# Tiles of the weight ring at 4224 instead of 4096 bytes, and two constants given up, in a decoder-block kernel

## The chip, the cores and the metric

The kernel runs on one core of one Trainium2 chip. The metric is the device time of one execution in microseconds (us), as the median over several executions. TensorE (PE) multiplies matrices, VectorE (DVE) and ScalarE (ACT) do elementwise work, GpSimd (POOL) a little of it, and SyncE (SP) issues every transfer (DMA) of this kernel. SBUF is the memory on the core, 128 partitions wide; an address below is a byte offset inside a partition, the same in all of them.

## The reference

One decoder block on x of 1024 tokens by 1024 channels, in float32. Two token mixers run side by side on the same normalised, modulated h: a chunked state-space mixer (SSD) and differential attention; two sigmoid gates merge them. A gated convolutional feed-forward part with 2816 hidden channels follows.

```python
h = rms_norm(x, pre_norm1_w) * (1.0 + sc1) + sh1
z, xbc, dt_raw, q, k, v, gates = jnp.split(h @ w_in, IN_SPLITS, axis=-1)
y_ssd = ssd_branch(z, xbc, dt_raw, ...)
y_att = diff_attention_branch(q, k, v, ...)          # softmax under a causal mask, blocks of 128 queries
gate_ssd, gate_att = jnp.split(sigmoid(gates), 2, axis=-1)
merged = gate_ssd * (y_ssd @ w_ssd_o) + gate_att * (y_att @ w_attn_o)
x = x + g1 * rms_norm(merged @ w_out, post_norm1_w)
h2 = rms_norm(x, pre_norm2_w) * (1.0 + sc2) + sh2
u_gate, u_val = jnp.split(causal_dwconv(h2 @ w_up, ...), 2, axis=-1)
x = x + g2 * rms_norm((gelu(u_gate) * u_val) @ w_down, post_norm2_w)
```

sh1, sc1, g1, sh2, sc2 and g2 are the six parts of silu(c) @ w_ada + b_ada.

## The kernel before

Every large product is made of three matmuls in the fp32r format: each operand is split into a high and a low part, and high times high, high times low and low times high are added up in PSUM. The big projections are arranged as block products with seven instead of eight multiplications (lists `order` and `downs`), so the same work is done with sums of blocks. One matmul has 128 rows by 128 columns of weights (the stationary operand, brought in by a weight load of its own) and streams 512 columns of the moving operand past them. In the z part (`mm3` at L954, printed on L118 to L120) it streams 346 or 348 columns.

**Memory.** Four pools share a partition, in this order. `cq` holds small constants. `wp` is the weight ring: a tag `wraw` with 3 buffers for weights as they are loaded, `whi` and `wlo` with 4 each for their split halves, 11 tiles of 4096 bytes. `sp` holds 43 slots of 4096 bytes, given out by the class `Slots` for activations, operands and scratch. `cp` holds the remaining constants. In the built program the ring's tiles start at 2048 + 4096 i and the slots at 47104 + 4096 k, so all of them start at multiples of 2048, and the 128-column pieces within them at multiples of 512. The exceptions are the z weights: a ring tile for them holds two rows of 346 (or 348) floats, one behind the other, so that the second starts 1384 (or 1392) bytes into the tile. For a part of them a tile `zown` of two slots stands in, where the second row starts 2048 bytes in.

**Order of the work.** PE, DVE, ACT and, until attention begins, SP have their order written out by hand in Python (`tc.manual_schedule`). In the part with attention (from L1674) SP is not in that list, and a scheduler sets the order of its transfers. PE's streams of matmuls are interleaved with attention by `fill(n)`, which emits n groups of three matmuls of a dense product.

**The mask.** `masked_min` (L1457) adds the causal mask to a tile of scores and takes the row minimum in one DVE instruction. Its mask `mw` is a slot with 896 zeros followed by a 128x128 block, 0 where a key may be seen and 1e30 elsewhere. That block is loaded early into a constant `maskbig` (L688) and copied into `mw` by DVE (L1681), just ahead of the first scores; the zeros are a memset (L1680).

**The gate rows.** `ada_turn` (L935) transposes two rows of gate factors on PE, copies them from PSUM into a constant `growt` of 16 partitions by 128 floats (L938) and writes them to DRAM as `rowd` (L940), from where they are later read broadcast over all partitions.

Of the kernel before, what the change touches and what calls it, by code (L numbers as in the profile page):

```python
# [17 lines left out]
P = 128  # L18
D = 1024
S = 1024  # L20
HALF = 512
KD = D // P
# [11 lines left out]
NROW = 48 + 256  # L34


class Slots:
    def __init__(self, pool, n):
        self.pool = pool
        self.free_list = list(range(n))  # L40
        self.of = {}
# [22 lines left out]
def kernel(ctx: ExitStack, tc: tile.TileContext, a: dict, out: bass.AP, dbg=None):  # L64
    nc = tc.nc
    V, A, G, T, SP = nc.vector, nc.scalar, nc.gpsimd, nc.tensor, nc.sync

    cq = ctx.enter_context(tc.tile_pool(name="cq", bufs=1))
    wp = ctx.enter_context(tc.tile_pool(name="wp", bufs=1))
    sp = ctx.enter_context(tc.tile_pool(name="sp", bufs=1))  # L70
    cp = ctx.enter_context(tc.tile_pool(name="cp", bufs=1))
    pp = ctx.enter_context(tc.tile_pool(name="pp", bufs=1, space=bass.MemoryType.PSUM))
# [1 line left out]
    SL = Slots(sp, NSLOT)  # L74

    def const(name, shape, dtype=F32):
        pool = cq if name in ("cT", "nhalf", "growt", "adac", "gcol", "aexp", "ssy") else cp
        return pool.tile(shape, dtype, tag=name, name=name)

    pairs_of_banks = ExitStack()  # L80
# [53 lines left out]
    def load_x(i):  # L134
        SP.dma_start(xts[i], a["x"][i * P : (i + 1) * P, :])

    cT = const("cT", [P, KD])
    nhalf = const("nhalf", [P, 8])
    ident = const("ident", [P, P])
    ones = const("ones", [P, P])  # L140
    tri = const("tri", [P, P])
    maskbig = const("maskbig", [P, P])
    SP.dma_start(cT, a["cT"])
    load_x(0)
    SP.dma_start(ident, a["ident"])
# [231 lines left out]
    def x_load():  # L377
        if not x_loads:
            return
        n, m = x_loads.pop(0)  # L380
        kind, i, j = pairs[m]
        src = {"gs": ("w_gate", "w_gate"), "xbc": ("w_xbc", "w_xbc"), "qk": ("w_q", "w_k"), "rope": ("w_q", "w_k")}[kind]["fv".index(n)]
        t = xw[n, m] = wp.tile([P, 2, KH, P], F32, tag="wraw", name=f"xw{n}{m}", bufs=3)
        SP.dma_start(t.rearrange("p h k c -> p (h k c)"), a[src][(i, j)["fv".index(n)]])
# [43 lines left out]
    n_ada, n_ald = 0, 0  # L428
    adac = const("adac", [P, 4 * KD])
    gcol = const("gcol", [P, 2 * KD])  # L430
    growt = const("growt", [2 * KD, P])
    sh2c, a2c = adac[:, KD : 2 * KD], adac[:, 2 * KD : 3 * KD]
    ada_of = {}

# [121 lines left out]
    with tc.manual_schedule(engines={EN.PE, EN.DVE, EN.Activation, EN.SP}):  # L556
# [128 lines left out]
                x_load()  # L685
        SP.dma_start(rows, a["rows"].broadcast_to([P, NROW]))
        SP.dma_start(tri, a["tri"])
        SP.dma_start(maskbig, a["maskbig"])  # L688
        x_load()
        SL.put(diag, *[t for p_ in adat for t in p_], rrow, raw3, *xT.values())  # L690
        vev1 = SL.get("vev1", F32, (P, 2, HALF))
# [148 lines left out]
    sm2 = SL.get("sm2", F32, (P, 1024))  # L840
    dtr, dt, la, acum, ea, cd, dte, sp0_ = (sm1[:, n] for n in range(8))
    sp1_ = sm2[:, 256:384]
    cbm = sm2[:, 384:640].rearrange("p (g l) -> p g l", g=2)
    btok = sm2[:, 640:896].rearrange("p (g l) -> p g l", g=2)
    ev = [SL.get(f"ev{i}", F32, (P, 2, HALF)) for i in range(3)]
# [2 lines left out]
    aexp = const("aexp", [P, NH])  # L848
# [94 lines left out]
    with tc.manual_schedule(engines={EN.PE, EN.DVE, EN.Activation, EN.SP}):  # L943
        for t_, (c0, wdt) in enumerate(thirds):
# [4 lines left out]
            for i in range(8):  # L949
# [20 lines left out]
                n = wdt - lo  # L970
# [52 lines left out]
    ssy = const("ssy", [P, 8, 2])  # L1023
# [9 lines left out]
    def run_bg(n):  # L1033
        for _ in range(min(n, len(bg))):
            tag, f_ = bg.popleft()
            f_()
            finished.add(tag)
# [67 lines left out]
    def fill(n):  # L1105
        for _ in range(n):
            next(stream, None)
# [110 lines left out]
    def turn_y(c, g, bank=ps_wb):  # L1218
        ps = bank(f"ytr{c}_{g}")
        for q in range(4):  # L1220
            T.transpose(ps[:, q * P : (q + 1) * P], yt[c % 3][:, (4 * g + q) * P : (4 * g + q + 1) * P], ident)
        st = yst[2 * (c == 7) + g]
        p4 = ps.rearrange("p (k t) -> p k t", t=P)
        s4 = st.rearrange("p (k n) t -> p k n t", n=2)
        A.activation(s4[:, :, 0, :], p4, AF.Copy)
        V.tensor_tensor(s4[:, :, 1, :], p4, s4[:, :, 0, :].bitcast(F32), op=ALU.subtract)
        SP.dma_start(ytd[:, 8 * g : 8 * g + 8, c * P : (c + 1) * P], st.bitcast(F32))
# [119 lines left out]
    mw = SL.get("mw")  # L1347
# [86 lines left out]
    def load_heads(j):  # L1434
        b = j % 2
        last = 2 + ((j + 1) * 96 - 1) // P
        if last > 3 and ("low", "w_k", last, 1) not in finished:
            run_lows()
            assert ("low", "w_k", last, 1) in finished
        assert emitted["scores"] >= 8 * (j - 1) and emitted["values"] >= 8 * (j - 1)  # L1440
        if j > 0:
            for s in range(2):
                load_highs(2 * j + s, qst[b][s], kst[b][s])
                load_lows(2 * j + s, klo[b][s])
        for kt in range(8):
            SP.dma_start(vt[b][:, kt, :], vd[kt][:, j * P : (j + 1) * P])
# [227 lines left out]
    with tc.manual_schedule(engines={EN.PE, EN.DVE, EN.Activation, EN.Pool}):  # L1674
        for n in range(NFIRST - 6):
            fill(1)
            if n == 1:
                turn_y(6, 1, ps_wc)
                load_heads(0)
                V.memset(mw[:, : S - P], 0.0)  # L1680
                V.tensor_copy(mw[:, S - P :], maskbig)  # L1681
            elif n == 8:
                turn_y(7, 0)
            elif n == 9:
                turn_y(7, 1, ps_wc)
            run_bg(1 if n < 8 else 2)
# [951 lines left out]
```

## Time and profile before

| | |
|---|---|
| median of 3 runs | 1803.32 us (1803.09 to 1804.15) |
| profiled execution | 1805.74 us, of which 1803.9 us are the span from first to last instruction |
| granted TensorE clock in it | 0.998 |
| DVE, ACT, POOL busy | 76%, 51%, 6% of the span |
| transfers | 356.18 MB, 59.7% of what 16 DMA engines could be busy |

The page gives busy time per engine, a chain of work that ended last, and groups of equal instructions with their mean length and the idle time ahead of them. PE's matmuls overlap each other in the records: a matmul of 512 columns is listed with 389 ns while the next one starts earlier, so the pace is read from start to start in the timeline, not from the mean length. The timeline has the time of start in us, the length in us, the engine, the line, the operation with output and inputs, its shape, and the idle time before it with what ended it.

### The profile page before, as it was taken

The page shows a single profiled execution, that of the slowest core. Times are in us where ns is not written, and L with a number is a line of the kernel's source. Part 1 is how long each engine was busy: PE and PEld are TensorE (multiplying, and loading weights), DVE is VectorE, ACT ScalarE, POOL GpSimd, SP SyncE. Part 2 cuts the span into 40 slices and gives each one's busy share as a digit, 9 for nine tenths or more (in the row PEclk, how much of TensorE's full clock was granted, in tenths as well). Part 3 has the DMA queues.
Part 4 walks back from the last instruction along what each step waited for, and adds up shares of the span by engine and source line. Part 5 has one row for each costly group of instructions (what it writes and reads, how often), then busy time and mean ns, then how long its engine had stood idle before and what let it go on. Part 6 is the DMA issues. An engine that isn't in the chain of part 4 may idle for free.

```text
span 1803.9 us, 24533 instructions
## 1 busy us (share of the span) xinstructions
PE 1780.5 (99%) x8749; PEld 1493.3 (83%) x8749; DVE 1363.7 (76%) x2245; ACT 919.6 (51%) x1794; POOL 111.7 (6%) x110
## 2 busy tenths in 40 slices
PE   8999999999999999999999999999999999999998
PEld 6788888899877888888888888888888888888887
DVE  7896888976489777666667876679898888876545
ACT  4454444443457556665555443665554554564532
POOL 0000000000155400000000000100000000000001
PEclk9999999999999999999999999999999999999999
DMA  9565687678877886679842576413232223378754
GB/s 368 180 221 164 244 273 258 188 240 279 267 257 245 256 246 175 174 208 272 262 147 100 181 252 254 154 53 117 99 125 103 100 100 111 122 240 305 232 161 165
DMA packets 165322, 356.18 MB, mean 197 GB/s; under 512 B 16064, under 2 KB 64976, under 8 KB 165200
## 3 DMA queue, kind: packets, MB, share of 16 engines
q1 hardware_dynamic: 165200, 354.62, 59.7%
q8 instruction: 69, 1.13, 0.3%
q14 instruction: 53, 0.43, 0.1%
HBM read 248.83 MB, written 103.62 MB: 195 GB/s over the span
## 4 chain that ended last, share of the span: by engine, by line
PE 62%; DVE 4%; ACT 3%; DMA 2%; issue 1%; SPq 0%; POOL 0%; DVEq 0%; POOLq 0%; ACTq 0%
PE upx L2026 4%; PE upx L2025 4%; PE upx L2027 4%; PE o L1532 2%; PE dx L2418 2%; PE dx L2416 2%; PE dx L2417 2%; PE upy L2025 2%; PE upy L2026 2%; PE upy L2027 2%; PE dy L2418 2%; PE dy L2416 2%; PE dy L2417 2%; PE at L1519 2%; PE mix L2088 1%; PE mix L2087 1%
## 5 line engine op out<-in xcount | busy, mean ns | idle before, releaser
L2025 PE MATMUL upx<-t,wu_t 128*128 128x512 f32 x264 | 103.1, 391 | 0.5 <-DVE cv L2481 0.4
L2026 PE MATMUL upx<-t,wu_t 128*128 128x512 f32 x264 | 102.8, 390 | 0.2 <-DVE t L2143 0.2
L2027 PE MATMUL upx<-t,wu_t 128*128 128x512 f32 x264 | 102.7, 389 | 0.0
L1457 DVE CUSTOM_DVE_ANT_0 sc<-sc,mw 128x256 f32<-128x256 f32 (+7 forms) x128 | 96.1, 771 | 8.5 <-PE sc L1470 7.3
L1999 ACT ACTIVATE wu_t<-sab 128x512 fp32r<-128x512 f32 x57 | 34.1, 627 | 127.5 <-DVE sab L2016 127.5
L1520 ACT COPY aT<-at 128x512 f32<-128x512 f32 (+2 forms) x96 | 45.9, 478 | 95.3 <-PE at L1519 95.0
L97 DVE TENSOR_TENSOR g_lo<-gst,g_hi 128x1024 fp32r<-128x1024 f32 (+1 forms) x42 | 47.4, 1134 | 49.0 <-ACT g_hi L96 49.0
L1532 PEld LDWEIGHTS o<-vt,aT 128*128 128x128 f32 x576 | 76.0, 191 | 7.2 <-ACT aT L1520 1.8
L1532 PE MATMUL o<-vt,aT 128*128 128x128 f32 x576 | 79.9, 275 | 1.3 <-ACT aT L1520 1.3
L96 ACT ACTIVATE g_hi<-gst 128x1024 fp32r<-128x1024 f32 (+1 forms) x42 | 41.3, 989 | 65.1 <-DMA gst<-gld_s 37.4
L398 ACT ACTIVATE xw_t<-xsab 128x512 fp32r<-128x512 f32 x45 | 27.3, 627 | 92.5 <-DVE xsab L407 92.5
L423 PE MATMUL xx<-xt,xw_t 128*128 128x512 f32 x180 | 70.2, 390 | 0.0
L424 PE MATMUL xx<-xt,xw_t 128*128 128x512 f32 x180 | 70.0, 389 | 0.0
L425 PE MATMUL xx<-xt,xw_t 128*128 128x512 f32 x180 | 70.0, 389 | 0.0
L1469 PE MATMUL sc<-kst,qst 128*128 128x512 f32 (+2 forms) x192 | 66.0, 352 | 0.0
L1507 DVE RECIPROCAL rsm<-ssum 128x2 f32<-128x2 f32 x64 | 10.6, 166 | 72.6 <-ACT p L1498 39.7
L1470 PE MATMUL sc<-klo,qst 128*128 128x512 f32 (+2 forms) x192 | 63.2, 346 | 0.0
L2043 DVE SCALAR_TENSOR_TENSOR ug<-cg,vec,ug 128x1023 f32<-128x1023 f32 (+1 forms) x44 | 56.3, 1279 | 6.1 <-ACT ug L2042 5.3
L2003 DVE TENSOR_TENSOR wu_t<-sab,wu_t 128x512 fp32r<-128x512 f32 x57 | 39.3, 689 | 26.5 <-ACT wu_t L1999 26.5
L2025 PEld LDWEIGHTS upx<-t,wu_t 128*128 128x128 f32 x264 | 49.6, 188 | 11.7 <-DVE cv L2481 1.4
L2026 PEld LDWEIGHTS upx<-t,wu_t 128*128 128x128 f32 x264 | 49.6, 188 | 10.6 <-DVE t L2143 0.5
L1511 DVE SCALAR_TENSOR_TENSOR p<-p,coef,p 128x512 f32<-128x512 f32 (+2 forms) x96 | 56.5, 616 | 2.2
(580 smaller groups left out, 5797.2 us busy)
## 6 DMA issues: line engine op xcount, KB each, us to landing
adas<-in_w_ada SPq DMA_DIRECT2D x32, 512.0 KB, 5.8
wdr<-in_w_down SPq DMA_DIRECT2D x22, 512.0 KB, 4.9
wtd<-wdr SPq DMA_DIRECT2D x22, 512.0 KB, 3.3
wuf<-in_w_up SPq DMA_DIRECT2D x22, 512.0 KB, 3.4
gld_s<-gsum SPq DMA_DIRECT2D x22, 512.0 KB, 2.8
gst<-gld_s SPq DMA_DIRECT2D x20, 512.0 KB, 4.8
wdt_raw<-wtd SPq DMA_DIRECT2D x20, 512.0 KB, 4.5
wuv<-in_w_up SPq DMA_DIRECT2D x19, 512.0 KB, 3.6
```

Source lines behind the costliest of these rows:

```text
L423: T.matmul(o, wh, xh_, start=(k == 0 and first), stop=False, skip_group_check=not first)
L424: T.matmul(o, wh, xl_, start=False, stop=False, skip_group_check=not first)
L425: T.matmul(o, wl, xh_, start=False, stop=(k == KH - 1), skip_group_check=not first)
L1457: V.tensor_tensor_reduce(out=sc, in0=sc, in1=mw[:, S - L :], scale=1.0, scalar=3.0e38, op0=ALU.add, op1=ALU.min, accum_out=col)
L1469: T.matmul(sc[:, n0:n1], qs_[s][:, tsl], ks_[s][:, n0:n1], start=True, stop=False)
L1532: T.matmul(po_of[j, grp][:, qi, :], at[:, k, :], vt[j % 2][:, kt, :], start=(kt == 0), stop=(kt == i))
L2025: T.matmul(out_, wh, xh_, start=(k == 0 and first), stop=False, skip_group_check=not first)
L2026: T.matmul(out_, wh, xl_, start=False, stop=False, skip_group_check=not first)
L2027: T.matmul(out_, wl, xh_, start=False, stop=(k == end), skip_group_check=not first)
L2416: T.matmul(o, gh[:, kk, tsl], wh, start=(k == 0 and not more), stop=False, skip_group_check=more)
L2417: T.matmul(o, gh[:, kk, tsl], wl, start=False, stop=False, skip_group_check=more)
L2418: T.matmul(o, gl[:, kk, tsl], wh, start=False, stop=(k == KF - 1), skip_group_check=more)
```

## The change

The ring's pool is wrapped in a class that makes every tile of it 1056 floats (4224 bytes) long and hands out a view of the front part in the wanted shape. Ring tile i now starts at 2048 + 4224 i, a multiple of 128 that is a multiple of 256 for every other tile. The slots follow it and start at 48512 + 4096 k, which is 128 bytes past a multiple of 256 for all 43. The 1408 bytes that this takes are found by giving up two constants of 512 bytes a partition and from what was free: the mask block has no constant of its own and is loaded by SP straight into `mw` where DVE copied it, and the gate rows use a free part of the slot `sm2`. The constant `tri` (a triangle of ones, used by the SSD part) moves to the pool ahead of the ring in place of `growt`.

```diff
+class Ring:
+    def __init__(self, pool):
+        self.pool = pool
+
+    def tile(self, shape, dtype, **kw):
+        n = math.prod(shape[1:])
+        t = self.pool.tile([P, D + 32], dtype, **kw)[:, :n]
+        return t.rearrange("p (a b) -> p a b", b=shape[2]) if len(shape) == 3 else t.rearrange("p (a b c) -> p a b c", b=shape[2], c=shape[3])
...
-    wp = ctx.enter_context(tc.tile_pool(name="wp", bufs=1))
+    wp = Ring(ctx.enter_context(tc.tile_pool(name="wp", bufs=1)))
...
-        pool = cq if name in ("cT", "nhalf", "growt", "adac", "gcol", "aexp", "ssy") else cp
+        pool = cq if name in ("cT", "nhalf", "tri", "adac", "gcol", "aexp", "ssy") else cp
...
-    maskbig = const("maskbig", [P, P])
...
-    growt = const("growt", [2 * KD, P])
...
-        SP.dma_start(maskbig, a["maskbig"])
...
+    growt = sm2[:, P : 2 * P]
...
-                V.tensor_copy(mw[:, S - P :], maskbig)
+                SP.dma_start(mw[:, S - P :], a["maskbig"])
```

On PE, ACT and POOL the instructions stand in the same order as before, with the same shapes. DVE and SP differ at the mask. These rows are DVE's ahead of the first masked scores (`sc`), before:

```order
L1226 TENSOR_TENSOR yst_3944<-ytr_1_5398,yst_3944 128x4x128
L1680 MEMSET mw 128x896
L1681 COPY mw<-maskbig 128x128
L152 TENSOR_SCALAR ssy<-ssy 128x2
L1199 SCALAR_TENSOR_TENSOR yt_3933<-yt_3933,ssy,nwr 128x512 x2
L1226 TENSOR_TENSOR yst_5365<-ytr_0_5445,yst_5365 128x4x128
L1226 TENSOR_TENSOR yst_5366<-ytr_1_5458,yst_5366 128x4x128
L1249 TENSOR_TENSOR w_k_lo<-w_k_raw,w_k_hi 128x512 x2
L1457 ISA sc_0_5476,nmx<-sc_0_5476,mw 128x128
```

The same place after the change, with the changed kernel's line numbers (`ISA` on L1465 is `masked_min`):

```order
L1234 TENSOR_TENSOR yst_3941<-ytr_1_5395,yst_3941 128x4x128
L1688 MEMSET mw 128x896
L161 TENSOR_SCALAR ssy<-ssy 128x2
L1207 SCALAR_TENSOR_TENSOR yt_3930<-yt_3930,ssy,nwr 128x512 x2
L1234 TENSOR_TENSOR yst_5362<-ytr_0_5442,yst_5362 128x4x128
L1234 TENSOR_TENSOR yst_5363<-ytr_1_5455,yst_5363 128x4x128
L1257 TENSOR_TENSOR w_k_lo<-w_k_raw,w_k_hi 128x512 x2
L1465 ISA sc_0_5473,nmx<-sc_0_5473,mw 128x128
```

Only the copy is gone; the first masked scores now wait for a transfer instead. On SP the same stretch reads as follows before, where `vt` are attention's value tiles, `ytd` the stores of turned SSD rows and `qd` stores of queries:

```order
L1227 DMA ytd<-yst_3944 128x8x128 [waits DMAHW4_49,DVE_49]
L1446 DMA vt_5367<-vd_165 128x128 [waits DMAHW5_49]
L1446 DMA vt_5367<-vd_166 128x128 [waits DMAHW6_49]
L1446 DMA vt_5367<-vd_167 128x128 [waits DMAHW7_49]
L1446 DMA vt_5367<-vd_168 128x128 [waits DMAHW0_49]
L1227 DMA ytd<-yst_5365 128x8x128 [waits DMAHW1_49,DVE_49]
L1227 DMA ytd<-yst_5366 128x8x128 [waits DMAHW2_49,DVE_49]
```

After the change:

```order
L1235 DMA ytd<-yst_3941 128x8x128 [waits DMAHW3_49,DVE_49]
L1454 DMA vt_5364<-vd_164 128x128 [waits DMAHW4_49]
L1454 DMA vt_5364<-vd_165 128x128 [waits DMAHW5_49]
L1454 DMA vt_5364<-vd_166 128x128 [waits DMAHW6_49]
L1454 DMA vt_5364<-vd_167 128x128 [waits DMAHW7_49]
L1689 DMA mw<-in_maskbig 128x128 [waits DMAHW0_49,PE_49]
L1235 DMA ytd<-yst_5362 128x8x128 [waits DMAHW1_49,DVE_49]
L1235 DMA ytd<-yst_5363 128x8x128 [waits DMAHW2_49,DVE_49]
```

The mask's transfer stands between the last value tile and the next store. It waits for the transfer eight places ahead of it and for the last matmul that read the slot `mw` is given. At two later places of attention the scheduler has put one load (of `w_q_raw`, of `qst`) some six transfers earlier.

## The prediction

> **What bounds the kernel now.** I began with the page: its span, busy times and chain of waits, then the groups of instructions by shape.
>
> ```profile
> span 1803.9 us, 24533 instructions
> PE 1780.5 (99%) x8749; PEld 1493.3 (83%) x8749; DVE 1363.7 (76%) x2245; ACT 919.6 (51%) x1794; POOL 111.7 (6%) x110
> PE 62%; DVE 4%; ACT 3%; DMA 2%; issue 1%; SPq 0%; POOL 0%; DVEq 0%; POOLq 0%; ACTq 0%
> L2027 PE MATMUL upx<-t,wu_t 128*128 128x512 f32 x264 | 102.7, 389 | 0.0
> ```
>
> PE is busy for 99% of the span: 1803.9 - 1780.5 leaves 23.4 us of standing still. The kernel is the sum of its matmuls, each at the pace at which PE takes the next one. The second view is a table of stretches: the start, the z products, and the middle of the up projection (after each engine's busy time stand the granted clock, the transfers' share and GB/s).
>
> ```profile
> 0.00:45.00 45.00, 38.89 (x188) 30.28 (x189) 32.20 (x64) 21.24 (x41) 2.24 (x6) 0.96 0.96 368
> 400.00:500.00 100.00, 99.55 (x607) 94.33 (x606) 60.62 (x114) 39.78 (x86) 10.59 (x9) 1.00 0.79 262
> 1300.00:1400.00 100.00, 100.00 (x442) 82.79 (x442) 87.22 (x116) 49.95 (x74) 0.00 (x0) 1.00 0.30 108
> ```
>
> Only at the start do transfers fill their time (0.96). Later PE never stands, at a full clock. In the timeline of PE in the up projection, twelve matmuls of 512 columns lie between these two starts:
>
> ```profile
> 1299.83 0.39 PE L2025 MATMUL upx<-t,wu_t 128*128 128x512 f32 x1
> 1302.55 0.39 PE L2025 MATMUL upx<-b,wu_b 128*128 128x512 f32 x1
> ```
>
> 2.72 / 12 = 226.7 ns each, which agrees with 100 us / 442 = 226.2. The program has 6384 fp32r matmuls of 512 columns, so they alone are 6384 x 226.7 ns = 1447 us. Whatever this change does to that pace decides its worth; everything else in it is a few instructions.
>
> **The change part by part.**
>
> *The copy that goes.* DVE's timeline around the mask:
>
> ```profile
> 637.32 0.16 DVE L1681 COPY mw<-maskbig 128x128 f32<-128x128 f32 x1
> 637.40 0.15 DVE L152 TENSOR_SCALAR ssy<-ssy 128x2 f32<-128x2 f32 x1
> 638.37 1.42 DVE L1199 SCALAR_TENSOR_TENSOR yt<-yt,ssy,nwr 128x512 f32<-128x512 f32 x2 [0.82 <-POOL ssy L153]
> 644.34 0.29 DVE L1457 CUSTOM_DVE_ANT_0 sc<-sc,mw 128x128 f32<-128x128 f32 x1
> ```
>
> Sixteen hundredths of a us go from DVE, which stands 0.82 us soon after, behind POOL. At most 0.16 us reaches PE through the normalised rows; PE has other matmuls queued there. I take 0, bounds -0.16 and 0.
>
> *The mask's transfer.* SP's timeline at its old place and at its new one:
>
> ```profile
> 70.67 0.43 SPq L688 DMA_DIRECT2D maskbig<-in_maskbig  x1
> 71.61 0.33 SPq L384 DMA_DIRECT2D xwv<-in_w_gate  x1
> ...
> 636.91 3.31 SPq L1446 DMA_DIRECT2D vt<-vd  x4
> 641.72 1.89 SPq L1227 DMA_DIRECT2D ytd<-yst  x2
> ```
>
> At 70.67 SP loses an issue of 0.43 us, but it stands from 71.10 to 71.61 ahead of the next load in any case: 0. At the new place the last value tile has been issued at 636.91 + 3.31 = 640.22; the mask's issue takes 0.43 and ends at 640.65, before the stores that wait for DVE until 641.72: 0 again. Those stores are what is queued behind the mask, so only a wait of the mask longer than 1.07 us would delay them. How long does the transfer take to land? The same 64 KB early in the kernel, the value tiles of the same size in the stretch 600 to 660 us, and the slowest group of loads in the transfers' table:
>
> ```profile
> L688 SPq DMA_DIRECT2D maskbig<-in_maskbig x1: 432/432/432, 70.7 to 70.7; - x1
> DMA to landing us min/median/max: 2.7/2.7/2.7
> ```
>
> ```profile
> L1446 SPq DMA_DIRECT2D vt<-vd x8: 319/430/1851, 612.6 to 639.8; - x8
> DMA to landing us min/median/max: 1.9/3.1/4.1
> ```
>
> ```profile
> qst<-qd SPq DMA_DIRECT2D x16, 512.0 KB, 8.8
> wv_raw<-in_w_v SPq DMA_DIRECT2D x7, 512.0 KB, 5.7
> wz_raw<-in_w_zdt SPq DMA_DIRECT2D x6, 346.0 KB, 5.1
> ```
>
> So the mask is there at 640.22 + 2.7 = 642.9 to 640.22 + 4.1 = 644.3, and DVE needs it at 644.34. Its own size is the nearest row, so I take 3.1: there at 643.3, 1.0 us early, cost 0. The far bound is the 8.8 us of a transfer eight times as large: 649.0, 4.7 us late. What waits behind masked_min is DVE's work on the scores, then PE on the turned probabilities:
>
> ```profile
> 646.90 0.30 PE L1519 MATMUL at<-ident,p 128*128 128x128 f32 x1 [0.42 <-DVE p L1511]
> ```
>
> PE already stands 0.42 us for them, so there is no cover: each us by which the mask is late is a us of the end.
>
> *The gate rows.* The same copy with the same shape goes to another place, and nothing else uses that part of `sm2`:
>
> ```profile
> 421.67 0.27 DVE L938 COPY growt<-adat 16x128 f32<-16x128 f32 x1
> ```
>
> The two stores after it stay. Cost 0; its own 0.27 us bounds it either way, and in this stretch PE is busy for 99.55 of 100 us.
>
> *The distance of the tiles.* All slots now begin 128 bytes past a multiple of 256, and half the ring's tiles too, so every one of the 6384 matmuls has an operand off the old grid. Before, all starts were multiples of 512 and the pace was 226.7, whichever tiles met. There is one exception to read a price from. In the z products a ring tile's second row starts 1384 (or 1392) bytes in, so half of the matmuls stream from an uneven start, while `zown` starts at even ones. PE's timeline, in three places, and the group:
>
> ```profile
> 390.34 0.32 PE L118 MATMUL z<-wz_hi,hT 128*128 128x346 f32 x1
> 392.24 0.32 PE L118 MATMUL z<-wz_hi,hT 128*128 128x346 f32 x1
> ...
> 410.30 0.32 PE L118 MATMUL z<-zown,hT 128*128 128x346 f32 x1
> 411.25 0.32 PE L118 MATMUL z<-wz_hi,hT 128*128 128x346 f32 x1
> 412.21 0.33 PE L118 MATMUL z<-wz_hi,hT 128*128 128x346 f32 x1
> ...
> 461.74 0.32 PE L118 MATMUL z<-wz_hi,b 128*128 128x348 f32 x1
> 464.58 0.32 PE L118 MATMUL z<-wz_hi,hT 128*128 128x348 f32 x1
> ```
>
> ```profile
> L120 PE MATMUL z<-wz_hi,hT 128*128 128x346 f32 x88 | 28.2, 320 | 0.0
> ```
>
> Twelve from the ring at 390.34 take 1.90 us, 158.3 ns each. Six from `zown` at 410.30 take 0.95, again 158.3. That is the plain comparison: no price. The six from the ring behind them take 0.96, 160.0; if that 1.7 ns were real, it would be 3.4 per uneven matmul. The 348 columns give eighteen in 2.84, 157.8. A column costs (389 - 320) / (512 - 346) = 0.416 ns by the groups' means; 226.7 less 164 columns is 158.5, so here the uneven half would gain 1.4 ns each, and 226.7 less 166 columns is 157.7, so at 346 it would lose 1.3 each. The bounds per uneven matmul are -1.4 and +1.3 from the longer stretches: 6384 x -0.0014 = -8.9 us and 6384 x 0.0013 = +8.3 us. The short stretch gives +21.7, the far end. I take 0, because the direct pair says so and because 128 is a rounder distance than 1384.
>
> What z does not show is a weight load from an uneven start, since its weights lie in slots. The nearest row is the up projection's: 82.79 us / 442 = 187 ns a load against a pace of 226.7, so some 39 ns of lengthening would be hidden. That cover is soft, as in the z stretch the same load is listed with 94.33 / 606 = 156 ns: a record may stretch to fill what there is. I take 0 here too.
>
> The Trainium skill, page "TensorE: Matmul & The Clock Gate", section "Part 2: What happens when you issue a matmul", says that TensorE reads weights and the moving operand through two separate ports, so that the load takes nothing from the running matmul. By it a new distance has no collision to take away; the trace agrees in so far as the pace is 158.3 for both kinds of start.
>
> *DVE and ACT on shifted tiles.* A write that starts 4 bytes off (`uv`) can be compared with an even one:
>
> ```profile
> L1511 DVE SCALAR_TENSOR_TENSOR p<-p,coef,p 128x512 f32<-128x512 f32 x48 | 35.4, 751 | 1.4
> L1511 DVE SCALAR_TENSOR_TENSOR p<-p,coef,p 128x384 f32<-128x384 f32 x16 | 9.8, 615 | 0.3
> L2043 DVE SCALAR_TENSOR_TENSOR uv<-cv,vec,uv 128x1023 f32<-128x1023 f32 x22 | 28.1, 1278 | 0.9 <-ACT uv L2042 0.9
> ```
>
> (751 - 615) / 128 = 1.06 ns per element between two even tiles, and (1278 - 751) / 511 = 1.03 on to the shifted one, so the offset costs nothing that shows: 0. In the up projection DVE has 12.8% of its time free as cover.
>
> *The transfers.* Lines of 346 floats land in uneven places too: 346 KB take 5.1 us and 512 KB 5.7. The difference of 166 KB in 0.6 us is 277 GB/s, about the 262 of that stretch, so uneven lines carry no visible surcharge: 0.
>
> *Sum.* All terms are 0, with -9 and +8 us from the pace as the wide bounds. The profiled execution has 1805.74 us (1803.9 and 1.84 outside the span), which is 2.42 above the median of 1803.32; the runs spread over 1803.09 to 1804.15. From the profiled 1805.74 the sum stays 1805.74, and from the median it stays **1803.3**.
>
> **The rivals.**
>
> *Slower: uneven reads cost PE.* If the 1.7 ns of the six matmuls at 411.25 is a price of uneven starts and not a wobble, each matmul pays 3.4 ns: +21.7, so 1825.0 us. At +1.3 ns, the price of the 346 row, it is 1811.6. It decides from 3.6 / 6384 = 0.56 ns a matmul. Against it stands the stretch at 390.34, equally uneven and not slower than `zown`. For it: a weight load from an uneven start is nowhere in the trace. Chance 0.10.
>
> *Faster: the even grid is itself a collision.* The 512 columns cost 512 x 0.416 = 213 ns of the 226.7; some 13.7 ns are fixed. If weight loads and streams collide because both start on one grid, a shift could free up to that: 6384 x 13.7 ns = 87 us, 1716 us. Against it: at z, 158.3 - 346 x 0.416 = 14.4 ns are fixed, for ring rows off the grid and for `zown` on it alike. Chance 0.06. A small gain of 1.4 ns, as the 348 row would have it, gives 1794.4; chance 0.05.
> The section "Back-to-back issue gap" of the same page of the Trainium skill gives N / 2.4 + 2.5 ns for a matmul in a warm stream, an estimated 215.8 ns for 512 columns. By it 10.9 ns of the 226.7 could go, an estimated 70 us.
>
> *The mask comes late.* At 4.1 us and with its issue's 0.43 ahead it lands at 644.75, 0.4 late; at 8.8 it is 4.7 late, 1808.0. The mean is some 2.5: 1805.8. Against it: transfers of this size nearby land in 3.1. Chance 0.05.
>
> *Transfers slow down because they start unevenly.* If each 4096-byte line costs an extra part, it is paid where transfers fill the time: 3% of 45 us at 0.96, +1.3 us, 1804.6; later the transfers' share leaves room. Against it stand the 346 KB loads. Chance 0.03.
> The Trainium skill, page "DMA: Bandwidth & Descriptors", section "How a descriptor splits into AXI transactions", speaks against this change: a descriptor that does not start on a multiple of 256 bytes begins its first read at the boundary below and pays for the bytes it does not use. For 128 bytes ahead of 4096 that is an estimated 3%, on every slot. The rows of the z weights do not show it.
>
> That the change does nothing at all is the forecast itself.
>
> **How the numbers follow.** About 0.2%, or 3.6 us, is what a measurement of this kernel can tell from no change. The forecast of no change has 0.71, and the two small rivals (mask 0.05, transfers 0.03) lie mostly within the same bound: same 0.79. The uneven reads make slower 0.10, the two cases of a freed collision faster 0.11. The range takes in the bounds of the pace, 1803.3 - 8.9 = 1794.4 to 1803.3 + 8.3 = 1811.6, and with them the small gain and the late mask. It leaves out the large gain (0.06) and the dear end of the slower rival (at most 0.10), 0.16 together.
>
> **What would show it right or wrong.** In the profile after, the table of stretches should give about 442 matmuls in 100 us of the up projection and twelve starts 2.72 us apart; 2.70 or 2.74 over many stretches would mean a price or gain of 1.7 ns and refute the main term. The z stretch should keep 158.3. The first masked_min should start near 644.3 and name PE or DVE, not a transfer, as what it waited for, with some 0.4 us of PE's wait behind it. PE's busy time in the first 45 us should stay near 38.9 with about 188 matmuls; clearly fewer would mean the transfers pay. I would be wrong altogether if PE's busy time left 1780 by over 4 us.

## The result

| | before | after |
|---|---|---|
| median | 1803.44 us (1803.09 to 1804.15) | 1821.30 us (1820.23 to 1822.95) |
| profiled execution | 1805.74 | 1820.23 |
| span in it | 1803.9 | 1818.5 |

The change makes the kernel slower by 17.9 us: the ratio is 1.0100, with an interval of 1.0085 to 1.0115 (four runs of each kernel). The two profiled executions differ by 14.5, because the one of before lies 2.3 above its median and the one of after 1.1 below its own. These are the page's busy times and the chain of waits of the changed kernel:

```profile
span 1818.5 us, 24532 instructions
PE 1795.6 (99%) x8749; PEld 1494.8 (82%) x8749; DVE 1364.4 (75%) x2244; ACT 920.5 (51%) x1794; POOL 111.8 (6%) x110
PE 65%; DVE 3%; ACT 2%; DMA 1%; issue 1%; POOL 0%; DVEq 0%; SPq 0%; POOLq 0%; ACTq 0%
```

PE has the same 8749 records and is busy for 15.1 us longer, which is all of the span's 14.6. DVE, ACT and POOL have not moved. Nobody waits more: the span less PE's busy time was 23.4 us and is 22.9. So the matmuls themselves have slowed down. The table of stretches, with the three places of the prediction:

```profile
0.00:45.00 45.00, 38.49 (x192) 30.58 (x193) 33.20 (x65) 21.47 (x41) 2.24 (x6) 1.00 0.97 372
400.00:500.00 100.00, 99.62 (x608) 95.06 (x607) 58.13 (x111) 38.20 (x82) 8.21 (x7) 1.00 0.79 262
1300.00:1400.00 100.00, 100.00 (x438) 81.98 (x437) 87.73 (x115) 50.79 (x75) 0.00 (x0) 1.00 0.32 111
```

The start and the z stretch are as before. In the up projection 438 matmuls take the 100 us that held 442, at a full granted clock and with PE never standing. PE's timeline there shows that not all of them are slower:

```profile
1300.12 0.39 PE L2033 MATMUL upx<-t,wu_t 128*128 128x512 f32 x1
...
1302.39 0.39 PE L2034 MATMUL upx<-t,wu_t 128*128 128x512 f32 x1
...
1302.85 0.40 PE L2033 MATMUL upy<-b,wu_b 128*128 128x512 f32 x1
1303.09 0.40 PE L2034 MATMUL upy<-b,wu_b 128*128 128x512 f32 x1
1303.32 0.39 PE L2035 MATMUL upy<-b,wu_b 128*128 128x512 f32 x1
...
1305.64 0.39 PE L2033 MATMUL upx<-t,wu_t 128*128 128x512 f32 x1
```

Ten matmuls from 1300.12 to 1302.39 take 2.27 us, 227.0 ns each, the old pace. The twelve from 1302.85 to 1305.64 take 2.79, 232.5 each, and their steps are uneven (0.24, 0.23). Length and shape are equal; only the tiles of weights and stream are others. I put each matmul's start beside the addresses that its operands have in the built program, and sorted the spacing by how far the next weights start from the streamed operand, modulo 256 bytes. This covers the runs of 512 columns without a wait:

```
                                  before            after
weights in ring, stream in slots
  alike                           3496   227.0 ns   1773   228.2 ns
  128 apart                          -              1732   232.8 ns
weights in slots, stream in ring
  alike                           1324   227.1 ns    649   230.8 ns
  128 apart                          -               675   231.1 ns
```

Since all slots stand at 128 modulo 256 and every other ring tile does too, half of the pairs are now apart. In the lower half of the table the streamed tile changes within every group of three, and both kinds are slow. A change of distance takes some matmuls to settle: in the up projection, where a run of pairs 128 apart gives way to a run of alike ones, the spacings are 236, 228, 233 and 231 ns before 226 and 227 return. The three dense streams account for most of the loss. Summed from each start to the next one, waits included, the up projection's spacings are 425.5 us after 420.8, the gate projection's 290.0 after 285.9, and the down projection's 213.4 after 209.2: +12.9 beside PE's +15.1.

### The profile page after: what moved, and what is told of

Read it like the earlier page. It is cut to its first block, busy times and chain, and to the rows that moved or that the text cites. A ratio compares the mean times of both kernels' runs of the same rounds, so it can differ in the third digit from the quotient of the medians.

```text
span 1818.5 us, 24532 instructions
## 1 busy us (share of the span) xinstructions
PE 1795.6 (99%) x8749; PEld 1494.8 (82%) x8749; DVE 1364.4 (75%) x2244; ACT 920.5 (51%) x1794; POOL 111.8 (6%) x110
## 4 chain that ended last, share of the span: by engine, by line
PE 65%; DVE 3%; ACT 2%; DMA 1%; issue 1%; POOL 0%; DVEq 0%; SPq 0%; POOLq 0%; ACTq 0%
PE upx L2033 4%; PE upx L2034 4%; PE upx L2035 4%; PE o L1540 3%; PE dx L2424 2%; PE dx L2425 2%; PE upy L2035 2%; PE upy L2033 2%; PE upy L2034 2%; PE dx L2426 2%; PE dy L2424 2%; PE dy L2425 2%; PE dy L2426 2%; PE at L1527 2%; PE mix L2094 1%; PE mix L2095 1%
## 5 line engine op out<-in xcount | busy, mean ns | idle before, releaser
L1465 DVE CUSTOM_DVE_ANT_0 sc<-sc,mw 128x256 f32<-128x256 f32 (+7 forms) x128 | 96.2, 772 | 8.4 <-PE sc L1478 7.2
L2033 PEld LDWEIGHTS upx<-t,wu_t 128*128 128x128 f32 x264 | 49.6, 188 | 11.8 <-DVE cv L2489 1.0
L2034 PEld LDWEIGHTS upx<-t,wu_t 128*128 128x128 f32 x264 | 49.7, 188 | 11.4 <-DVE t L2151 0.5
L2035 PEld LDWEIGHTS upx<-t,wu_t 128*128 128x128 f32 x264 | 49.6, 188 | 10.9
```

The lines of the kernel that those rows point to most:

```text
L1465: V.tensor_tensor_reduce(out=sc, in0=sc, in1=mw[:, S - L :], scale=1.0, scalar=3.0e38, op0=ALU.add, op1=ALU.min, accum_out=col)
L2033: T.matmul(out_, wh, xh_, start=(k == 0 and first), stop=False, skip_group_check=not first)
L2034: T.matmul(out_, wh, xl_, start=False, stop=False, skip_group_check=not first)
L2035: T.matmul(out_, wl, xh_, start=False, stop=(k == end), skip_group_check=not first)
```

## The experiments

Three theories stood at first. **P**: a matmul of 512 columns is dear when its weights and its streamed operand start 128 bytes apart modulo 256. **U**: uneven starts are dear by themselves. **R**: the loss comes from the rest of the change. Ratios below are against runs of the kernel before on the same chip.

**slots128**, slots shifted alone. The kernel before with one edit, an unused tile ahead of the slots:

```diff
+    sp.tile([P, 32], F32, tag="gap_sp", name="gap_sp")
```

> The kernel before with 128 unused bytes between ring and slots: ring tiles stay at multiples of 2048, every slot lies 128 bytes past a multiple of 256. Theory P (phase: a matmul is dear when its weights and its moving operand start 128 bytes apart modulo 256, by 6 ns): all 5520 matmuls of 512 columns between ring and slots are apart, 5520 x 6 ns = +33 us, 1836 us; up, gate and down projections all near 233 ns. Theory U (unevenness: each uneven start costs, the more uneven operands the more): one uneven operand in each, fewer than after the change, so less than its +18 us. Theory R (the rest: the mask's transfer or the gate rows): 1803.

Measured 1829.71 us against 1803.47, ratio 1.0148 (1.0132 to 1.0163): +26.2 us with every tile spacing of the old kernel and the old mask. Its order of instructions on all engines is that of before. The spacing is 232.4 ns for ring weights and 233.2 for slot weights. This speaks for P, though the total is some 7 us short of its 33; U's bound, less than after, fails. The stretch and PE's line on the page:

```profile
1300.00:1400.00 100.00, 100.00 (x433) 81.26 (x432) 86.70 (x114) 50.35 (x74) 0.00 (x0) 1.00 0.32 111
```

```profile
PE 1806.1 (99%) x8749; PEld 1495.7 (82%) x8749; DVE 1364.8 (75%) x2245; ACT 920.1 (50%) x1794; POOL 111.4 (6%) x110
```

433 matmuls where there were 442, and PE is busy for 25.6 us more than before.

**both128**, ring and slots shifted together. The same line, but in the pool ahead of the ring:

```diff
+    cq.tile([P, 32], F32, tag="gap_cq", name="gap_cq")
```

> The kernel before with 128 unused bytes ahead of the ring: ring tiles and slots all lie 128 bytes past a multiple of 256. Theory P: weights and moving operands start alike modulo 256, so 1803 us and 226.7 ns. Theory U: two uneven operands in each of 5520 matmuls, at least the cost of the change's half-uneven ring, 1821 us or more. Theory R: 1803.

Measured 1805.00 against 1803.47, ratio 1.0008 (0.9998 to 1.0018). Everything is uneven, and the pace is the old one:

```profile
1300.00:1400.00 100.00, 100.00 (x442) 82.80 (x442) 87.25 (x116) 50.54 (x75) 0.00 (x0) 1.00 0.31 108
```

U falls. A start off the grid costs nothing if both operands share it.

**slots256**, the gap ahead of the slots doubled to 64 floats.

> The kernel before with 256 unused bytes between ring and slots: the two start 256 bytes apart modulo 512, but alike modulo 256. Theory P with a period of 256: 1803 us. With a period of 512 or more: some of the 33 us of the 128-byte gap, above 1815. Theory U and theory R: 1803.

Measured 1803.22, ratio 0.9999 (0.9989 to 1.0008); 227.0 and 227.1 ns. The relation has a period of 256 bytes, or of a whole fraction of 256.

**mask_only**, the change without the class around the ring.

```diff
-    wp = Ring(ctx.enter_context(tc.tile_pool(name="wp", bufs=1)))
+    wp = ctx.enter_context(tc.tile_pool(name="wp", bufs=1))
```

> The changed kernel without the class around the ring: the mask's transfer, the gate rows in a slot and the moved constant stay, all tiles are at multiples of 2048 again. Theory P and theory U: 1803 us within 0.1%. Theory R: all of the +18 us, 1821.

Measured 1804.45, ratio 1.0005 (0.9996 to 1.0015). R falls: mask, gate rows and the moved constant are worth nothing that can be measured.

**after_even**, the changed kernel with the slots put back to multiples of 256 by the same gap line (`gap_sp`, 32 floats).

> The changed kernel with 128 unused bytes between ring and slots: every slot is at a multiple of 256 again, the ring stays as changed, half of its tiles at uneven multiples of 128. Theory P: the other half of the weights is apart from the slots now, as many as before the edit, 1821 us, and the dear matmuls are those with weights at 128 or 384 modulo 512. Theory U: only half of the ring's starts are uneven now instead of all the slots too, so clearly less than half of the +18 us, under 1812.

Measured 1822.13, ratio 1.0104 (1.0087 to 1.0121), as slow as the change itself, with far fewer uneven starts. Ring weights at the slots' distance take 228.5 ns, those 128 apart 232.8: the dear tiles have changed places, as P has it.

**slots64**, the gap cut to 16 floats.

> The kernel before with 64 unused bytes between ring and slots, so weights and moving operands start 64 bytes apart modulo 128. Theory P as it stands (two halves of 128 bytes, the price is that of standing in opposite halves): half of a matmul's reads are in opposite halves, some 13 us, 1816. Theory B (blocks of 64 bytes or less whose order decides; any shift but a multiple of 256 breaks the pattern): the full price of the 128-byte gap, 1829. If only a shift of exactly 128 costs: 1803.

Measured 1821.35, ratio 1.0101 (1.0086 to 1.0116). The two directions differ: with weights in the ring, 64 bytes behind the stream, the spacing is 229.0 ns; with weights in slots, 64 ahead, it is 233.3, the full price. So P's two halves of 128 bytes are not the whole story, and neither is theory B, which wanted the full price both ways.

**scan32**, ring tiles 32 bytes further apart than before (the change's class with `D + 8`).

> The kernel before with ring tiles 4128 bytes apart, so the eight tiles of split halves have eight different starts against the slots, all multiples of 32 bytes modulo 256. To be read from the trace by pairs: the spacing of matmuls in the up, gate and down projections against the distance of weights and moving operand. Theory P: 227 ns at 0, 233 at 128, in between at the others, the same on both sides. Theory B: 227 at 0 alone and 232 to 234 at the seven others. If a distance under 226.7 exists, a kernel faster than before can be built on it.

Measured 1835.03, one run. Spacing where the weights of two neighbouring matmuls, both in the ring, have the same distance from the stream:

```
weights minus stream, mod 256      0     32     64     96    128    160    192    224
mean spacing, ns               228.7  233.0  233.6  233.5  233.3  233.5  229.5  233.3
matmuls                          391    361    371    382    346    345    335    346
```

Zero is the steady pace (most are 226 or 227; the mean holds some that are still settling). One other distance, 64 behind, costs 2 to 3 ns; the other six cost all of it. This settles for theory B with one exception that I can't explain. The mean of no distance is below 226.7, so the old layout already has the best of these eight, and nothing faster than before can be built on them. Distances between multiples of 32 bytes were not tried.

Why then did the z products, 104 and 112 bytes apart, show no such price? **cols** shortens two of three matmuls, each stream to another width, here the up projection:

```diff
-            T.matmul(out_, wh, xl_, start=False, ...
-            T.matmul(out_, wl, xh_, start=False, ...
+            T.matmul(out_[:, :508], wh, xl_[:, :508], start=False, ...
+            T.matmul(out_[:, :508], wl, xh_[:, :508], start=False, ...
```

> The kernel before, in which the second and third of each group of three matmuls stream fewer columns: 508 in the up projection, 448 in the gate projection, 480 in the down projection (the last columns of the two correction terms are left out, so the output is less exact there). Tiles lie as before, all alike modulo 256. At 2.4 columns per ns and 13.3 ns fixed a group would take 226.7 + 2 x 225.0 = 676.7 ns (225.6 a matmul), 626.7 (208.9) and 653.3 (217.8). Theory L (the steady pace needs streams of whole 256 bytes, which is why the z products with 346 columns could not show the price): the gate projection with 448 columns = 7 x 256 bytes stays steady at 208.9; up with 508 and down with 480 get the wobbling spacing and about +6 ns, 231 and 224. Theory C (columns don't matter): 225.6, 208.9 and 217.8, all steady.

**cols_slots128** adds the gap of 128 bytes.

> The same with 128 unused bytes between ring and slots, so that weights and moving operands are apart. Theory L: the gate projection gets dearer by about 6 ns, 215; up and down, already out of step, change by under 2 ns, as the z products did with the change. Theory C: all three get 5 to 6 ns dearer.

Here are the mean spacings of the three matmuls of a group. The first column is an estimate: the 226.7 ns of 512 columns less the columns left out, at 2.4 columns per ns (0.416 ns a column in the prediction's rows).

```
                            steady, est.     alike   128 apart
up, 512 and 2 x 508              225.6       233.3     228.6
gate, 512 and 2 x 448            208.9       213.1     211.4
down, 512 and 2 x 480            217.8       220.1     222.2
```

Theory C falls at once: all three streams are slower than its figures though no tile has moved. L falls in its detail, as 448 columns are whole 256 bytes and are dear too. And the gap is no longer a price: in two of three streams it is a gain. The whole kernel took 1802.88 us beside 1802.92 of before, and 1800.24 with the gap, one run each, though the columns left out would have taken PE an estimated 32.7 us by 2.4 columns per ns (616 x 8, 420 x 128 and 308 x 64 of them). Two thirds of that are seen again in the spacing: 1848 x 7.7 + 1260 x 4.2 + 924 x 2.3 ns = 21.6 us. Part of the rest went into waits for DVE that before does not have, 2.8 us in the gate projection and 2.7 us in the down projection.

The 233.3 ns of the up projection are an average of two paces. PE's timeline of cols has twelve matmuls, tiles alike, in 2.72 us at one place and in 2.83 us at another:

```profile
1200.02 0.39 PE L2025 MATMUL upy<-t,wu_t 128*128 128x512 f32 x1
...
1202.74 0.39 PE L2025 MATMUL upx<-t,wu_t 128*128 128x512 f32 x1
...
1300.35 0.40 PE L2025 MATMUL upx<-t,wu_t 128*128 128x512 f32 x1
...
1303.18 0.40 PE L2025 MATMUL upy<-b,wu_b 128*128 128x512 f32 x1
```

Of 607 groups of three, 147 take 678 to 682 ns, all of them before 1266 us, and 450 take 706 or 707, all after it. Widths, lines and distances modulo 256 are the same in both. So in mixed widths the distance does not fix the spacing by itself; what decides between the two paces is not known. The gap also changed pairs that it leaves alike: 381 of these spacings belong to weights in slots, and their mean went from 233.2 to 227.7 ns.

Mixed widths and short widths were still one thing. **even_cols** gives all three the same short width, except for the first matmul of a sum, and **even_cols_slots128** adds the gap. These two kernels leave the last columns of the three products out, so their output is not the block's; they serve to time matmuls only.

```diff
+            c = HALF if k == 0 and first else 448
-            T.matmul(o, wh, xh_, start=(k == 0 and first), ...
+            T.matmul(o[:, :c], wh, xh_[:, :c], start=(k == 0 and first), ...
```

> The kernel before with one shorter width for all three matmuls of a group: 508 columns in the up projection, 448 in the gate projection, 346 (the width of the z products) in the down projection; only the first matmul of a sum keeps 512, and the last columns of the products are left out. Tiles as before, all alike modulo 256. At 2.4 columns per ns and 13.3 ns fixed: 225.0, 200.0 and 157.5 ns. Theory L2 (the steady pace belongs to equal widths of whole 256 bytes; what failed in the mixed widths was the mixing): gate steady at 200.0; up and down wobble, 228 or more and 158.5 to 161. Theory L3 (512 alone is steady, any other width is out of step even when equal): gate 202 to 205 too. Theory C: all steady at the three figures.

> The same with 128 unused bytes between ring and slots. Theory L2: gate dearer by 4 to 7 ns, up by under 2, down by under 2 (with 346 columns the shift hardly shows, which is how the z rows misled). Theory L3: no column count but 512 shows the shift by more than 2 ns. Theory C: 5 to 6 ns on all three.

```
                    steady, est.     alike   128 apart
up, 508                 225.0        227.9     228.6
gate, 448               200.0        204.2     203.9
down, 346               157.5        159.5     159.2
```

The table holds spacings between two matmuls of the short width, without those across a wait. In the up projection a fifth of the pairs have weights in slots and stay alike under the gap; the others alone go from 227.9 to 228.7. From 1600 to 1700 us, with the down projection, the granted clock was 0.93 in both runs; some spacings of 287 to 291 ns there are left out of its row.

PE's timeline in the gate projection of even_cols, twelve matmuls of 448 columns, and twelve of even_cols_slots128:

```profile
262.36 0.37 PE L424 MATMUL xx<-xt,xw_t 128*128 128x448 f32 x1
...
264.84 0.37 PE L424 MATMUL xy<-hT,xw_b 128*128 128x448 f32 x1
```

```profile
262.43 0.36 PE L426 MATMUL xy<-xt,xw_t 128*128 128x448 f32 x1
...
264.87 0.37 PE L426 MATMUL xx<-xt,xw_t 128*128 128x448 f32 x1
```

2.48 us for tiles alike and 2.44 for tiles apart. L3 holds in what it says of the shift: at the three other widths tried, a stream lies 1.7 to 4.2 ns above the estimated steady figure wherever its tiles lie, and a gap of 128 bytes changes that by 0.8 ns at most. It does not hold in saying that every other width is out of step. The twelve alike matmuls above go 207, 207, 206 ns in turn, as regular as the old 227, 227, 226; 123 of 349 groups in this projection do. That regular pace is the dearer one: the others take 604 to 617 ns a group instead of 620. Theories L2 and C fall. The whole kernels took 1756.97 and 1766.56 us, one run each. As a control, 512 columns in another place of these same runs (the attention output, which the edit does not touch) still show the price; PE's timeline of even_cols, then of even_cols_slots128:

```profile
1010.15 0.39 PE L1643 MATMUL aox<-aot,wao_t 128*128 128x512 f32 x1
...
1012.87 0.39 PE L1643 MATMUL aox<-aot,wao_t 128*128 128x512 f32 x1
```

```profile
1009.71 0.39 PE L1644 MATMUL aoy<-aob,wao_b 128*128 128x512 f32 x1
...
1012.51 0.39 PE L1644 MATMUL aoy<-aob,wao_b 128*128 128x512 f32 x1
```

Twelve take 2.72 us with tiles alike, 226.7 ns each, and 2.80 apart, 233.3.

## Why the prediction was wrong

**The step that failed is the price of the tiles' distance, read from the z products.** The prediction compared 158.3 ns for ring rows with 158.3 for `zown` and took that for "no price". It was a true reading of a place where the price could not show. Streams of 346 columns take nearly the same with tiles alike and with tiles 128 bytes apart (159.5 ns in even_cols, 159.2 in even_cols_slots128), so the even `zown` was no clean reference. The z products of before say so themselves when all of them are sorted by address: at 346 columns 158.3 ns for pairs alike and 159.6 for uneven ones, at 348 columns 159.0 and 156.8, a price one way and a gain the other. The up projection's steady pace was the special case among the widths seen: 512 columns and equal starts modulo 256. The prediction had a hint in its hands. In the three dense streams of 512 columns nearly all steps before were 226 or 227 ns; at 346 they went from 153 to 169 for even rows and from 154 to 165 for uneven ones. A place that wobbles anyway can't price the loss of steadiness. Nor is 128 harmless for being "a rounder distance than 1384": in scan32 it costs what 32 or 96 cost.

**The forecast of no change** and its bounds (-1.4 and +1.3 ns a matmul) fell with that step. In fact a pair that is apart pays 5.4 to 6.1 ns in a long run of such pairs (slots128), and of the 5520 matmuls between ring and slots 2764 are apart now. Alike pairs that stand among them pay too, as the table of spacings shows: 1732 x 5.8 + 675 x 4.0 ns = 12.7 us for pairs apart and 1773 x 1.2 + 649 x 3.7 ns = 4.5 us for alike ones. Their sum is 17.2 us; PE's busy time grew by 15.1 and the medians by 17.9.

**The slower rival** had the right engine and side, and the condition from which it decides, 0.56 ns, was well exceeded. Its mechanism was wrong: starts off the grid cost nothing when both operands are (both128). It is the distance between the two operands that counts. That its 3.4 ns for each of 6384 matmuls, +21.7 us, came near the measured 17.9 was luck: it read them from six z matmuls, where no price can be told from the wobble, and the real price is near 6 ns for about half of the pairs. Its other argument, that no weight load from an uneven start was in the trace, was the better warning.

**The faster rival** asked whether the even grid is a collision. It is the reverse: of eight distances none is under 226.7 ns. The estimated 215.8 of the Trainium skill, "TensorE: Matmul & The Clock Gate", section "Back-to-back issue gap", is reached by no stream of 512 columns here. That section calls its formula the gap of a single, isolated matmul, which the prediction did not say.

**Two ports.** The same page's "Part 2: What happens when you issue a matmul" says that a weight load takes nothing from the running matmul. No run here separates the load from the stream, but the spacing depends on the distance between the addresses that the two read, which that sentence would not lead one to expect. Where in the chip they meet is open.

**The mask** went as forecast. SP's and DVE's timelines after, and the transfer's own time:

```profile
640.51 3.84 SPq L1454 DMA_DIRECT2D vt<-vd  x4
644.45 0.38 SPq L1689 DMA_DIRECT2D mw<-in_maskbig  x1
645.39 2.06 SPq L1235 DMA_DIRECT2D ytd<-yst  x2
```

```profile
DMA to landing us min/median/max: 3.4/3.4/3.4
```

```profile
646.81 1.28 DVE L1257 TENSOR_TENSOR w_k_lo<-w_k_raw,w_k_hi 128x512 fp32r<-128x512 f32 x2
648.01 0.29 DVE L1465 CUSTOM_DVE_ANT_0 sc<-sc,mw 128x128 f32<-128x128 f32 x1
```

The last value tile was issued by 644.35, the mask right behind it, and the stores still waited until 645.39. The mask landed at 644.45 + 3.4 = 647.85, where 3.1 us had been taken, and `masked_min` started at 648.01 without a wait, behind the same DVE work as before. The margin was 0.2 us instead of 1.0, and mask_only, at 1.0005 of before, agrees with a cost of zero.

**Gate rows, transfers, DVE and ACT** cost nothing, as forecast. Transfers at the start moved 372 GB/s after 368, with all slots 128 bytes past a multiple of 256, so the surcharge of the Trainium skill's "DMA: Bandwidth & Descriptors", section "How a descriptor splits into AXI transactions", does not show. These are loads, which write the slots, while the section speaks of where a read starts; what a store that reads a slot costs was not measured by itself. DVE's total is 1364.4 us after 1363.7 with one copy fewer.

**Open:** why 64 bytes behind costs 2 to 3 ns and 64 ahead all 6; what meets what at the memory; why mixed widths with equal distances keep two paces; and what widths other than 512, 508, 448 and 346 do.

## What to carry to other kernels

When a price is to be read from another place of the trace, ask first whether that place could show it: a clean pace (226 and 227 alone) and a wobbling one (153 to 169) are two regimes, and here only the first had something to lose. Where a stream of fp32r matmuls of 512 columns runs at a perfectly regular step, treat its operand addresses as part of the tuning, and when tiles are padded keep weights and stream alike modulo 256 bytes. A regular step is no proof of the best one: at 448 columns it was 206.7 ns, and the uneven groups beside it took 201 to 206 ns a matmul. Sorting start-to-start spacing by the operands' addresses found in one trace what means by line had blurred.

## What the runs showed of the hardware

- In a long run, fp32r matmuls of 512 columns start 226.7 ns apart when the weights and the streamed operand begin alike modulo 256 bytes, whether both at a multiple of 256 or both 128 past one (both128). At six of seven other multiples of 32 bytes it is 233 to 233.6 (scan32), and with the weights 64 behind 229 to 229.5 (slots64, scan32).
- Out of step, the steps repeat in a cycle rather than scatter: 226, 229, 232 ns in slots64 with ring weights; 238 and 229 in turn in the down projection of slots128; and a cycle of seven, 232, 241, 232, 231, 232, 228, 230, in its up projection.
- Fewer columns need not be faster. With all tiles alike, groups of 512, 508 and 508 columns took 680 ns in 147 of 607 cases and 706 or 707 in 450, where 512, 512 and 512 take 680 (cols).
- At the other widths tried, the shift by 128 bytes has no price: 448 columns take 204.2 ns for tiles alike and 203.9 for tiles apart (even_cols, even_cols_slots128).
